# Register-addressed key page fetches on GpSimd, and a later place for the first memory weight's split

## The chip, the core and the metric

The kernel runs on one core of a Trainium2 chip. The metric is the device time of one execution in microseconds (us). A core has a matrix engine (TensorE, PE in the profile; its weight loads are PEld), a vector engine (VectorE, DVE), an activation engine (ScalarE, ACT), GpSimd (POOL), and SyncE (SP), which in this kernel only issues transfers. Each engine works through its own queue in order. The order of each queue is fixed when the program is built, and engines wait for one another by semaphores. Transfers between the main memory and the on-chip memory run on 16 DMA engines and are issued here from SP, POOL and in a few cases ACT.

## The reference: one decoder layer for a prompt and eight samples

A layer of a decoder is computed for a prompt of 512 tokens and for one new token of each of eight sequences that have 1024 cached tokens. What matters here:

```
past = cache_kv_l[page_table]                     # nsa_sample: 8 pages of 128 tokens for each sequence
full = jnp.concatenate([past, new4], axis=1)
kvc = compress_blocks(full[:, :, 0:2], w_cmp, pe_cmp)
...
s_c = jnp.einsum('btghd,bngd->bghtn', qg, kvc[:, :, 0]) * scale      # compressed branch
o_c = jnp.einsum('bghtn,bngd->btghd', p_c.astype(dt), kvc[:, :, 1])
...
o_s = jnp.einsum('bghtkr,bgtkrd->btghd', p_s..., sel[..., 1, :])     # selected branch
...
def mem_project(mem, g_mem, w_xkv):
    return (rmsnorm(mem, g_mem) @ w_xkv).reshape(B, M, 2, X_HEADS, X_HEAD_DIM)
```

The cached keys of a sequence lie in pages in any order, and the page table names them. The attention has a compressed, a selected and a window branch. The memory projection multiplies 256 memory tokens with `w_xkv`; its keys and values are used by the cross-attention of a later stage. A gated feed-forward part follows.

## The kernel before

The work goes in stages. First come the input projections of the normalised tokens (`project`, line 205) with the rounding of each weight into two parts, `w_hi` by ACT and `w_lo`, the difference, by DVE (`split_w`, lines 191 to 195, whose copies are recorded as lines 117 and 120). Between and behind these come the scores of the cached keys (`cached_scores`, from line 658), the sample's softmaxes, the compressed values (`cmp_values`, from 812), the selected values (`selected_values`, from 870) and the pooling group (`pooling`, from 981). From about 174 us on the prompt's attention runs beside the rest of the memory projection and part of the output projection, then cross-attention and the feed-forward part, which takes the larger half of the time.

Several such streams are written as generators, and `merge` takes from them in turn by given weights. This gives the order of the program. A scheduler in the framework then orders each engine's queue when the program is built: of what its own model of the time holds ready, it takes what comes first in the program. `tc.high_priority()` moves instructions ahead, and `tc.issue_after(i)` adds for each instruction of a block on i's engine that it stands behind i in that engine's queue; it adds no semaphore.

*Key pages.* `fetch_keys(b)` (line 327) fetches the keys of sequence b: eight pages, each 128 partitions with 1 KB. For six of the eight sequences SP loads the page numbers from the tile `pages` into registers, with bounds, and issues eight direct transfers with the page number in a register (line 335). For sequences 1 and 2 POOL issues eight indirect transfers (line 337). Those take a row number for each partition from the tile `ix_k`, which DVE works out from the page table and a constant (`row_numbers`, line 323). In the program 0 comes first, then 2, 1 and, in between other work, 3 to 7. Sequence 2's fetch stands under `issue_after(last_square)`, an ACT instruction. The keys of sequences 0 to 3 are first read by `cached_scores(0)` (line 668), those of 4 to 7 by `cached_scores(1)`. POOL also fetches rows of cached values, in the indirect form (`fetch_values`, line 344, tiles `Vcmp` and `Vslc`, row numbers `ix_v`), and stores the first keys and values (line 487).

*Compressed values.* `cmp_values` goes in four rounds q. Each has products with the cached values (line 826), a copy of the result (`pvs`; by DVE for even q, by ACT for odd), four transposes (834), a copy of those (`pv2`, in the profile `pv`; by ACT for even q, by DVE for odd) and products with the compression weight (844). `cmp_last` keeps the last instruction of ACT and of DVE up to that copy, and after the fourth round it names those of that round. The scaling of the memory tokens (`memory_split`, line 1216, tiles `mT_hi`, `mT_lo`) already stands behind these two.

*Memory keys.* `memory_keys(q, banks)` (line 1223) loads a quarter of the key weights, rounds it in two halves with `split_w` and multiplies it (line 1235). Quarter 0 is called at the end of `pooling`, which runs beside `sample_end`. Its buffer `w_raw` is one of two that all weights take in turn, so its transfer (line 181) starts when the weight before has been split. Before the change only the second half of quarter 2 had an order by hand:

```
with tc.issue_after(reduced[0]) if reduced and q == 2 and l else ExitStack():
    w = split_w(raw[:, :, l * P:(l + 1) * P])
```

## Time and profile before

| what | value |
|---|---|
| median of 3 runs | 836.8 us (834.53 to 836.95) |
| the profiled execution's own time | 842.45 us |
| its span, from the first to the last instruction | 840.6 us |
| its mean granted TensorE clock | 0.991 |
| busy in the span: PE, PEld, DVE, ACT, POOL | 813.0, 757.0, 605.4, 448.0, 104.3 us |
| moved by DMA | 137.87 MB, 164 GB/s on the mean |
| POOL indirect transfers of key pages | 16, 1116 ns each on the mean |

A row of a timeline has the start and the duration in us, the engine, the line of the kernel, the operation, the tiles (written <- read), the shape, and how often it is repeated. Brackets at the end give the idle time of the engine just before, and what ended it. "SPq" is the queue that issues transfers. In the chain of waits a row has a start, a duration and what the chain went through. A row of the stage table has a stretch, its length and, for each engine, busy time and number of instructions. "issue" is time in which an engine waited for nothing that the profile shows, "remote" a wait whose releaser it does not know.

### The profile page before, as it was taken

The page shows a single profiled execution, that of the slowest core. Times are in us where ns is not written, and L with a number is a line of the kernel's source. Part 1 is how long each engine was busy: PE and PEld are TensorE (multiplying, and loading weights), DVE is VectorE, ACT ScalarE, POOL GpSimd, SP SyncE. Part 2 cuts the span into 40 slices and gives each one's busy share as a digit, 9 for nine tenths or more (in the row PEclk, how much of TensorE's full clock was granted, in tenths as well). Part 3 has the DMA queues.
Part 4 walks back from the last instruction along what each step waited for, and adds up shares of the span by engine and source line. Part 5 has one row for each costly group of instructions (what it writes and reads, how often), then busy time and mean ns, then how long its engine had stood idle before and what let it go on. Part 6 is the DMA issues. An engine that isn't in the chain of part 4 may idle for free.

```text
span 840.6 us, 17844 instructions
## 1 busy us (share of the span) xinstructions
PE 813.0 (97%) x6889; PEld 757.0 (90%) x6889; DVE 605.4 (72%) x1460; ACT 448.0 (53%) x940; POOL 104.3 (12%) x100
## 2 busy tenths in 40 slices
PE   8889998999999999999999999999999999999996
PEld 7878785887778799999899999999999999999995
DVE  6454395798676767888864599988888888887623
ACT  6543135667765545344444365676665665655542
POOL 2330011000000014000022000211111211200021
PEclk9999999999999999999999999999999999999998
DMA  9976975673321175477624323766686776763422
GB/s 329 251 241 168 400 300 185 206 254 126 102 75 40 38 215 190 133 250 250 204 64 110 92 68 110 162 152 133 152 166 139 158 158 138 149 154 108 168 121 102
DMA packets 146365, 137.87 MB, mean 164 GB/s; under 512 B 6416, under 2 KB 133264, under 8 KB 144088
## 3 DMA queue, kind: packets, MB, share of 16 engines
q1 hardware_dynamic: 127224, 114.63, 43.9%
q0 software_dynamic: 18624, 21.26, 12.1%
q8 instruction: 54, 0.88, 0.4%
q10 hardware_dynamic: 432, 0.84, 0.3%
q14 instruction: 31, 0.25, 0.1%
HBM read 129.56 MB, written 10.69 MB: 167 GB/s over the span
## 4 chain that ended last, share of the span: by engine, by line
PE 84%; DVE 7%; DMA 3%; ACT 2%; issue 2%; another core or an unknown queue 0%; SPq 0%; DVEq 0%; ACTq 0%
PE ps_pp L205 26%; PE ps_pp L1829 15%; PE ps_pp L1890 15%; PE ps_tb L1266 2%; PE ps_o L1158 2%; PE ps_pp L2070 2%; PE ps_t L1890 2%; PE ps_tb L1075 2%; PE ps_sc L1111 2%; PE ps_tf L1143 2%; PE ps_x L1467 1%; PE ps_tb L1235 1%; PE ps_x L1488 1%; DVE w_lo L120 1%; DMA w_raw<-in_w_xkv_dram 1%
## 5 line engine op out<-in xcount | busy, mean ns | idle before, releaser
L1890 PE MATMUL ps_pp<-xm,w_hi 128*128 128x260 f32 x720 | 133.3, 285 | 0.1
L1890 PEld LDWEIGHTS ps_pp<-xm,w_hi 128*128 128x128 f32 x720 | 110.9, 188 | 2.3 <-ACT ext L117 0.3
L117 ACT ACTIVATE w_hi<-w_u 128x512 fp32r<-128x512 f32 (+2 forms) x110 | 72.7, 661 | 66.5 <-PE ps_pp L1890 22.7
L1890 PE MATMUL ps_pp<-xm,w_lo 128*128 128x260 f32 x360 | 101.4, 282 | 0.0
L120 DVE TENSOR_TENSOR w_lo<-w_u,w_hi 128x512 fp32r<-128x512 f32 (+2 forms) x110 | 80.1, 729 | 16.6 <-ACT w_hi L117 15.3
L1890 PEld LDWEIGHTS ps_pp<-xm,w_lo 128*128 128x128 f32 x360 | 67.7, 188 | 0.0
L120 DVE TENSOR_TENSOR hT<-hT,ps_pp 128x520 f32<-128x520 f32 (+1 forms) x44 | 28.3, 644 | 45.0 <-PE ps_pp L205 18.0
L205 PE MATMUL ps_pp<-x_hi,w_hi 128*128 128x260 f32 x288 | 60.0, 286 | 0.0
L205 PE MATMUL ps_pp<-x_hi,w_lo 128*128 128x260 f32 x288 | 59.6, 285 | 0.0
L205 PE MATMUL ps_pp<-x_lo,w_hi 128*128 128x260 f32 x288 | 58.4, 284 | 0.0
L117 ACT ACTIVATE w_hi<-w_raw 128x1024 fp32r<-128x1024 f32 (+1 forms) x38 | 35.0, 922 | 42.2 <-PE ps_pp L205 30.6
L205 PE MATMUL ps_pp<-xn_hi,w_hi 128*128 128x260 f32 x208 | 46.4, 300 | 1.9 <-issue 1.0
L205 PE MATMUL ps_pp<-xn_lo,w_hi 128*128 128x260 f32 x208 | 44.5, 293 | 2.6 <-issue 2.4
L1880 POOL DMA_DIRECT2D w_u<-in_w_up_dram x19 | 24.4, 1285 | 179.5 <-DMA w_u<-in_w_up_dram 106.4
L205 PEld LDWEIGHTS ps_pp<-x_hi,w_lo 128*128 128x128 f32 x288 | 44.9, 188 | 0.6 <-issue 0.4
L205 PE MATMUL ps_pp<-xn_hi,w_lo 128*128 128x260 f32 x208 | 44.2, 293 | 1.3 <-DVE w_lo L120 0.8
L205 PEld LDWEIGHTS ps_pp<-x_hi,w_hi 128*128 128x128 f32 x288 | 44.9, 188 | 0.3
L205 PEld LDWEIGHTS ps_pp<-x_lo,w_hi 128*128 128x128 f32 x288 | 44.5, 188 | 0.4 <-issue 0.4
L1121 ACT ACTIVATE prob<-prob,mx 128x384 f32<-128x384 f32 (+3 forms) x64 | 35.4, 555 | 17.7 <-DVE mx L1119 17.4
L120 DVE TENSOR_TENSOR w_lo<-w_raw,w_hi 128x1024 fp32r<-128x1024 f32 (+1 forms) x38 | 41.4, 1089 | 4.2 <-ACT w_hi L117 3.9
L120 DVE TENSOR_TENSOR w_lo<-raw_x,w_hi 128x512 fp32r<-128x512 f32 (+1 forms) x53 | 35.7, 674 | 10.3 <-ACT w_hi L117 9.6
L117 ACT ACTIVATE w_hi<-raw_x 128x512 fp32r<-128x512 f32 (+1 forms) x53 | 32.8, 619 | 18.2 <-PE ps_pp L1890 13.1
(495 smaller groups left out, 2321.7 us busy)
## 6 DMA issues: line engine op xcount, KB each, us to landing
w_u<-in_w_up_dram SPq DMA_DIRECT2D x57, 256.0 KB
xkr<-in_cache_mem_dram SPq DMA_DIRECT2D x16, 512.0 KB
xvr<-in_cache_mem_dram SPq DMA_DIRECT2D x16, 512.0 KB
raw_x<-in_w_up_dram SPq DMA_DIRECT2D x26, 256.0 KB
Kt<-in_k_t_dram SPq DMA_DIRECT2D x48, 128.0 KB
w_u<-in_w_up_dram SPq DMA_DIRECT2D x10, 512.0 KB
w_u<-in_w_down_dram SPq DMA_DIRECT2D x20, 256.0 KB
w_u<-in_w_up_dram POOLq DMA_DIRECT2D x19, 256.0 KB
```

The lines of the kernel that those rows point to most:

```text
L117: act.activation(o, i, AF.Copy, scale=scale)
L120: (eng or dve).tensor_tensor(o, a, b, op=op)
L205: pe.matmul(o, a[:, k, :], x[:, hf, :], start=(k == 0 and j == 0), stop=(k == kt - 1 and j == 2))
L1075: pe.matmul(ps[:, :HT], a[:, k, :], y[x][:, k, hf, :], start=(k + j == 0), stop=(k == 3 and j == 2))
L1111: pe.matmul(ss_[hl][:, 0:n], Qst[:, h, qc], k[:, g, u, 0:n], start=(u == 0), stop=(u == 1), skip_group_check=True)
L1121: act.activation(p[:, 0:nk], p[:, 0:nk], AF.Exp, bias=mx[:, hh:hh + 1], scale=-1.0, accum_out=sm[:, hh:hh + 1])
L1143: pe.transpose(pt[:, hh * P:(hh + 1) * P], pr[hh][:, kb * P:(kb + 1) * P], ident)
L1158: pe.matmul(po[hp * 64:(hp + 1) * 64, g * 256:(g + 1) * 256], Vtok[:, br, kb, g * 64:(g + 1) * 64], pTs[kb][:, hp * 256:(hp + 1) * 256], s ...
L1266: pe.matmul(ps[i], x[:, k, ts_], w[:, kl, :], start=(k == 0 and j == 0), stop=(k == KT - 1 and j == 2))
L1829: pe.matmul(ps[:, hf, :HT], a[:, k, :], x[:, hf, :], start=(k0 + k + j == 0), stop=(k0 + k == kt - 1 and j == 2))
L1880: pool.dma_start(u[1], b, accum_op=OP.add)
L1890: pe.matmul(ps, a[:, i, :], b, start=(first and i + q == 0), stop=(i == NI - 1 and q == 2), skip_group_check=True)
```

## The change

Two things. The keys of sequences 1 and 2 are fetched by POOL in the form that SP uses: POOL loads the eight page numbers into registers of its own, with the same bounds, and issues eight direct transfers for each sequence. `ix_k` and its DVE operation are gone; `ix_v` stays. And both halves of the split of the first quarter of the memory weight are placed behind the instructions in `cmp_last`, ACT's part behind ACT's and DVE's part behind DVE's. The order that quarter 2 had by hand stays.

```diff
-    ix_k = const.tile([P, 64], I32, name="ix_k")
     ix_v = const.tile([P, 4], I32, name="ix_v")
...
     def row_numbers():
-        for o, i, n, f, c in ((ix_k, pages[:, 0:64], 64, float(P), C_IX), (ix_v, pages[:, 64:68], 4, 8.0, C_IX + 1)):
-            dve.scalar_tensor_tensor(o, i, f, cst[:, c:c + 1].to_broadcast([P, n]), op0=OP.mult, op1=OP.add)
+        dve.scalar_tensor_tensor(ix_v, pages[:, 64:68], 8.0, cst[:, C_IX + 1:C_IX + 2].to_broadcast([P, 4]), op0=OP.mult, op1=OP.add)
 
     def fetch_keys(b):
 
         t = (pair_tile if b < 2 else ring_tile)("Kt").rearrange("p (a x) -> p a x", a=NPG)
-        if b not in (1, 2):
-            _, at = nc.values_load_multi_w_load_instructions(pages[0:1, b * NPG:(b + 1) * NPG], engines=(EN.SP,),
-                                                             min_val=0, max_val=NPHYS - 1)
+        en, q = (EN.Pool, pool) if b in (1, 2) else (EN.SP, sp)
+        _, at = nc.values_load_multi_w_load_instructions(pages[0:1, b * NPG:(b + 1) * NPG], engines=(en,),
+                                                         min_val=0, max_val=NPHYS - 1)
         for a in range(NPG):
-            if b not in (1, 2):
-                sp.dma_start(t[:, a], A["k_t"][bass.ds(at[a], 1)].rearrange("o p x -> (o p) x"))
-                continue
-            pool.indirect_dma_start(out=t[:, a], out_offset=None, in_=A["k_t"].rearrange("n p x -> (n p) x"),
-                                    in_offset=bass.IndirectOffsetOnAxis(ap=ix_k[:, b * NPG + a:b * NPG + a + 1], axis=0))
+            q.dma_start(t[:, a], A["k_t"][bass.ds(at[a], 1)].rearrange("o p x -> (o p) x"))
         Kt[b] = t
...
         for l in range(2):
-            with tc.issue_after(reduced[0]) if reduced and q == 2 and l else ExitStack():
+            with ExitStack() as late_:
+                for i in (reduced if q == 2 and l else cmp_last.values() if q == 0 else ()):
+                    late_.enter_context(tc.issue_after(i))
                 w = split_w(raw[:, :, l * P:(l + 1) * P])
```

## The prediction

> **What bounds the kernel now.** I read the page first: the span and the shares of the chain that ended last.

> ```profile
> span 840.6 us, 17844 instructions
> ...
> PE 84%; DVE 7%; DMA 3%; ACT 2%; issue 2%; another core or an unknown queue 0%; SPq 0%; DVEq 0%; ACTq 0%
> ```

> TensorE carries the chain, so a time in which TensorE stands still is lost time, and a time in which another engine waits is not. Next I asked for the busy time of every engine by stage (columns: stretch, its length, then busy time and number of instructions of PE, PEld, DVE, ACT, POOL, then granted TensorE clock, DMA share, GB/s).

> ```profile
> 124.00:175.00 51.00, 46.17 (x502) 37.74 (x491) 35.54 (x109) 29.06 (x53) 6.95 (x9) 0.97 0.62 202
> 175.00:430.00 255.00, 252.06 (x1943) 219.02 (x1942) 191.02 (x623) 136.52 (x321) 15.88 (x17) 1.00 0.46 147
> ```

> From 175 us on TensorE idles 2.9 us in 255 (255.00 - 252.06). Everything the diff touches lies before that, where there is something to win: 4.8 us idle between 124 and 175, with the clock not fully granted. So I went into that stage with the chain of waits and the timeline of ScalarE (ACT).

> ```profile
> 123.76 1.15 DVE w_lo L120
> 124.92 8.62 DMA w_raw<-in_w_xkv_dram
> ```

> ```profile
> 128.93 0.67 ACT L117 ACTIVATE pl_d<-ps_pp,vec 128x520 f32<-128x520 f32 x1
> 133.65 1.06 ACT L117 ACTIVATE w_hi<-w_raw 128x1024 fp32r<-128x1024 f32 x1 [4.04 <-DMA w_raw<-in_w_xkv_dram]
> 134.61 0.58 ACT L117 ACTIVATE pv<-ps_tb 128x512 f32<-128x512 f32 x1
> ```

> This is the stall that the second half of the diff aims at. The first memory weight is asked for at 124.92, when a buffer came free, and takes 8.62 us. Its rounding (w_hi) stands in ACT's queue ahead of the copy pv of the compressed values. ACT sits idle for 4.04 us, and pv sits behind it. The timeline of TensorE shows what that costs:

> ```profile
> 130.97 0.63 PE L834 MATMUL ps_tb<-cst,pvs 128*128 128x128 f32 x4
> ...
> 131.53 1.06 PE L826 MATMUL ps_tb<-Vcmp,PTc 128*32 128x512 f32 x8
> ...
> 135.24 0.66 PE L844 MATMUL ps_s<-pv,wv 128*64 128x32 f32 x16 [2.65 <-ACT pv L117]
> ...
> 136.50 1.05 PE L834 MATMUL ps_tb<-cst,pvs 128*128 128x128 f32 x4
> ...
> 137.49 1.94 PE L826 MATMUL ps_tb<-Vcmp,PTc 128*32 128x512 f32 x8
> ```

> The source of pv (L834) was done at 131.60. TensorE waited for pv until 135.24, 2.65 us with nothing to do, and then ran the next L834 and L826 in 1.05 and 1.94 us where the same groups had taken 0.63 and 1.06. The granted clock says why:

> ```profile
> 25.00:29.20 4.20, 1.18 (x7) 0.70 (x5) 1.21 (x10) 0.00 (x0) 2.00 (x3) 1.00 1.05 201
> 30.20:33.60 3.40, 3.40 (x18) 3.40 (x17) 1.97 (x6) 2.22 (x3) 0.00 (x0) 0.50 1.02 276
> 45.00:48.40 3.40, 3.40 (x30) 3.40 (x29) 3.13 (x8) 2.79 (x8) 2.79 (x3) 1.00 1.03 333
> 49.20:53.30 4.10, 0.00 (x0) 0.00 (x0) 0.71 (x2) 0.00 (x0) 2.46 (x3) 1.00 0.61 193
> 54.10:57.50 3.40, 3.40 (x17) 3.05 (x15) 2.68 (x4) 3.31 (x8) 0.00 (x0) 0.50 0.83 250
> 132.60:135.20 2.60, 0.00 (x0) 0.00 (x0) 1.57 (x7) 1.55 (x3) 0.00 (x0) 1.00 0.71 294
> 136.00:139.40 3.40, 3.40 (x16) 1.41 (x16) 0.69 (x1) 1.72 (x4) 0.00 (x0) 0.50 0.02 5
> ```

> Three times TensorE stands still for 2.6 to 4.1 us, and each time 3.4 us at half clock follow. Two of the three lie before 60 us, beside POOL work.

> **Part two of the change, the weight behind the compressed values.** It removes the wait of 2.65 us: pv can start when L834 ends, and TensorE has its own work until 132.59 (131.53 + 1.06). If the idle goes, I count the half clock behind it as gone too: 0.42 on L834 (1.05 - 0.63) and 0.88 on L826 (1.94 - 1.06), 1.30 together. So 3.95 us in all.

> [...] The row has a half clock behind 2.6 idle us.

> What it adds: w_hi (1.06 on ACT) and its difference w_lo (1.22 on DVE) now run behind the last copies of the compressed values, at a place where both engines feed the selected branch. These rows show that place:

> ```profile
> 141.76 1.22 DVE L120 TENSOR_TENSOR w_lo<-w_raw,w_hi 128x1024 fp32r<-128x1024 f32 x1
> ...
> 142.99 0.94 POOL L344 DMA_INDIRECT Vslc<-in_v_slc_dram,ix_v  x1 [15.04 <-PE ps_tb L826]
> 143.46 2.91 ACT L128 ACTIVATE mT_hi<-mt,vec 128x256 fp32r<-128x256 f32 x7
> ...
> 151.44 0.42 DVE L114 COPY PTs<-ps_tb 128x256 f32<-128x256 f32 x1 [1.16 <-PE ps_tb L865]
> ...
> 156.65 1.29 ACT L117 ACTIVATE Ksl<-zk 64x512 fp32r<-64x512 f32 x2 [5.27 <-PE ps_s L874]
> 156.74 0.29 DVE L114 COPY oS<-ps_s 128x128 f32<-128x128 f32 x1 [4.21 <-PE ps_s L874]
> ...
> 158.46 0.28 PE L1235 MATMUL ps_pp<-mT_hi,w_hi 128*128 128x256 f32 x1
> ```

> The first product that needs the weight (L1235) starts at 158.46, and before that ACT idles 5.27 and DVE 4.21 us: room for 1.06 and 1.22 at no cost. If the scheduler puts them ahead of the PTs copies instead, those are up to 1.22 us later and TensorE waits that long. Both ends are possible; I take 0.30, near the free end, because the memory scaling (mT) and the PTs copies come earlier in the program and the idle is four times the work. The fetch at 142.99 is released by TensorE (L826) and moves forward with it, so it is not late next. Sum: 3.95 - 0.30 = 3.65 us won; ends 1.43 (2.65 - 1.22) and 3.95.

> **Part one, the key pages.** Removed: one DVE operation and sixteen indirect transfers. Added: on POOL, a wait for the page table, a load of eight page numbers with bounds for each of two blocks, and sixteen direct transfers. No direct POOL transfer with a register stands in this trace; the nearest rows are POOL's plain store (L487) and SP's own fetches with a register (L335), whose queue the change does not touch.

> ```profile
> 15.99 0.22 DVE L325 SCALAR_TENSOR_TENSOR ix_k<-pages,cst 128x64 int32<-128x64 int32 x1
> ...
> 16.50 2.15 POOL L337 DMA_INDIRECT Kt<-in_k_t_dram,ix_k  x1 [15.23 <-DVE ix_k L325]
> ...
> 39.63 0.58 POOL L487 DMA_DIRECT2D out_kv_t_dram<-Vtok  x1 [12.03 <-DVE Vtok L120]
> 40.52 0.99 POOL L337 DMA_INDIRECT Kt<-in_k_t_dram,ix_k  x1 [0.30 <-issue]
> ...
> 50.59 0.94 POOL L337 DMA_INDIRECT Kt<-in_k_t_dram,ix_k  x1 [0.30 <-issue]
> ...
> 18.11 0.56 SPq L406 DMA_DIRECT2D WT<-in_w_cmp_e_dram  x1
> 24.84 9.03 SPq L335 DMA_DIRECT2D Kt<-in_k_t_dram  x8
> ...
> 72.47 1.44 PE L668 MATMUL ps_s<-Kt,QW 128*32 128x64 f32 x88
> ```

> Dearest case for a block: SP's first one, 6.2 us of loading (18.67 to 24.84) and 9.03 of issuing. Two such on POOL after 15.99 end at 46.5 (15.99 + 2 x 15.2). Cheapest: 16 x 0.58 = 9.3 us. Today the second set ends at 51.53 (50.59 + 0.94), and the first reader, L668, comes at 72.47 with no wait for it. So both ends are hidden behind 20 us of cover; only beyond that would it cost a microsecond for each microsecond. Behind POOL's new wait stand the kv store and the transfers, and only L668 waits for those. I take 0 for the issue itself, and 0 for the DVE operation (0.22 beside a TensorE that goes on working).

> **The sum.** The profiled execution took 842.45 us, 1.85 more than its span; 842.45 - 3.65 = 838.8. The three times have a median of 836.8 (834.53 to 836.95), so the profiled one is 5.65 slower; the wait on a weight's arrival has no reason to differ, and I take the difference from the median: 836.8 - 3.65 = 833.15, say **833.1**. About 0.3%, 2.5 us here, is what a measurement can tell from no change.

> **Rivals.**
> *B, the early stalls go too.* These two rows belong to the second one:

> ```profile
> 52.59 0.70 DVE L120 TENSOR_TENSOR ztile<-ps_pp,R 128x520 f32<-128x520 f32 x1 [4.03 <-remote]
> 53.34 0.33 PE L574 MATMUL ps_pp<-xn_hi,wg_hi 128*56 128x260 f32 x1 [4.17 <-DVE ztile L120]
> ```

> The DVE waits 4.03 us for something that the profile cannot name, while POOL's second set of indirect transfers (40.52 to 51.53) runs; the stall at 25 to 29.2 lies beside the first set. If dropping the indirect form cures both, it is 3.02 (4.20 - 1.18) and 4.10 idle, and at half clock 18 and 17 instructions ran where 30 do, 1.36 and 1.47: 9.95 us. Against it: the transfers stay on POOL, in bursts of eight, and the profiled execution is 5.65 slower than the median, so part of these stalls may not exist in the timed runs. Half of it, 5.0, gives 833.15 - 5.0 = 828.2; all of it 823.2. [...] Chance 0.19.
> *C, the order does not do what it says.* The edges only set a place in two queues; the scheduler may put another waiting operation there, or both parts' effects cancel: 836.8. Chance 0.18.
> *E, the wait goes and the half clock stays.* Its 3.4 us follow a wait shorter than they are, so it may have another cause: 2.65 - 0.30 = 2.35, 834.45. [...] Chance 0.10.
> *D, slower: the second block's pages come into the loading rush.* Nothing ties them to the kv store at 39.63; without the index operation they may follow the first set at once.

> ```profile
> 31.49 1.23 DVE L120 TENSOR_TENSOR w_lo<-w_q,w_hi 128x1024 fp32r<-128x1024 f32 x1 [5.18 <-ACT w_hi L117]
> ...
> 36.06 0.40 PE L205 MATMUL ps_pp<-xn_hi,w_hi 128*128 128x260 f32 x2
> ```

> Between 25 and 29.2 the DMA is full at 201 GB/s. One more MB ahead of the query weight costs 5.2 us; that weight is ready at 32.72 and needed at 36.06, so 3.3 are covered and 1.9 are not. If the timed runs lack the stall at 25 us, TensorE is there 4.4 us earlier (3.02 + 1.36) and 6.3 are not covered, with 1.36 of half clock behind them: 833.15 + 7.7 = 840.8. It decides from 3.3 us of delay on; what speaks against it is that today's second set waited too. Chance 0.17.

> **How the numbers follow.** Forecast A, 833.1, has 0.36 (835.4 to 832.9 by its own ends). Faster by over 2.5 us (under 834.3): B and nine tenths of A, 0.52. Within: C, E and the rest of A, 0.31. Slower: D, 0.17. The range reaches from 826.0, between half and the whole of B's price, to 840.0, short of D's dearest; about 0.18 is left out.

> **What would show it.** Right: no idle before L844 of the compressed values, w_hi of the memory weight after the last pvs, granted clock 1.00 around it, ACT's 4.04 gone; transfers L332 as direct ones on POOL that end before 52 us; L668 without a wait. B shows as busy TensorE between 25 and 54 us at full clock, D as a w_q that lands later and a TensorE that waits for its w_lo near 36 us. I am wrong if another wait stands ahead of pv, or if the PTs copies come a microsecond later than TensorE asks for them.

## The result and the profile after

The changed kernel took 827.11 us (median of 5 runs, 826.34 to 830.93), the kernel before 834.53 us (5 runs on the same chip, 832.31 to 836.95). The ratio is 0.9914, with a 95% interval of 0.9885 to 0.9942: 7.2 us faster, between 4.8 and 9.6. The forecast was 833.1 us, with a range of 826.0 to 840.0. Two executions of experiments further below (1568.84 us of first_indirect, 2734.39 us of second_indirect) lie far above all others, and the ratios are those of the runs without them.

The profiled execution took 830.93 us, against 842.45 before. These are the span and the shares of the chain that ended last, on its page:

```profile
span 829.3 us, 17914 instructions
...
PE 85%; DVE 4%; DMA 4%; ACT 3%; issue 1%; SPq 1%; DVEq 0%; POOL 0%; ACTq 0%
```

DVE's share has fallen from 7% to 4%, and "issue" from 2% to 1%. Next come the stretches that were asked of the kernel before, and three new ones around 90 us, with the same columns:

```profile
25.00:29.20 4.20, 4.20 (x38) 4.20 (x37) 3.48 (x18) 2.77 (x3) 0.60 (x2) 1.00 1.01 211
30.20:33.60 3.40, 3.40 (x29) 3.21 (x28) 1.74 (x4) 2.15 (x3) 0.00 (x0) 1.00 1.05 339
45.00:48.40 3.40, 3.39 (x26) 3.19 (x27) 2.58 (x3) 3.33 (x6) 0.00 (x0) 1.00 1.06 384
49.20:53.30 4.10, 4.10 (x33) 3.68 (x32) 0.84 (x2) 0.48 (x2) 0.00 (x0) 1.00 0.52 142
54.10:57.50 3.40, 3.40 (x25) 2.88 (x26) 0.58 (x3) 0.76 (x4) 0.00 (x0) 1.00 0.33 87
84.00:89.40 5.40, 4.22 (x36) 4.13 (x35) 2.48 (x5) 1.55 (x2) 1.77 (x2) 1.00 1.00 416
89.40:92.40 3.00, 0.33 (x3) 0.12 (x2) 0.00 (x0) 0.00 (x0) 0.00 (x0) 1.00 1.00 415
92.40:95.80 3.40, 3.29 (x16) 0.59 (x16) 0.00 (x0) 0.00 (x0) 0.00 (x0) 0.51 1.02 429
```

Both early stalls are gone. From 25.0 to 29.2 TensorE is busy for all 4.20 us, where it was busy for 1.18, and from 49.2 to 53.3 for all 4.10, where it did nothing. Both half clocks behind them are gone too. But there is a new hole from 89.4 to 92.4 with half clock behind it, while the DMA engines are full at 415 GB/s. The timeline of GpSimd shows the new transfers:

```profile
21.00 4.07 POOL L332 DMA_DIRECT2D Kt<-in_k_t_dram  x7 [19.60 <-DMA xrow_s<-in_x_row_s_dram]
25.47 0.54 POOL L332 DMA_DIRECT2D Kt<-in_k_t_dram  x1 [0.41 <-issue]
34.30 0.55 POOL L481 DMA_DIRECT2D out_kv_t_dram<-Vtok  x1 [8.29 <-DVE Vtok L120]
34.91 4.63 POOL L332 DMA_DIRECT2D Kt<-in_k_t_dram  x8
```

Eight direct transfers take 4.63 us (0.58 each, the value of the plain store that I had set as the cheap end). Eight indirect ones had taken 11.1 us (16.50 to 27.60). The second set ends at 39.54.

The third part is the compressed values, first on the timeline of TensorE, then ScalarE's copy and rounding:

```profile
125.22 1.06 PE L820 MATMUL ps_tb<-Vcmp,PTc 128*32 128x512 f32 x8
126.22 0.66 PE L838 MATMUL ps_s<-pv,wv 128*64 128x32 f32 x16
127.27 0.60 PE L828 MATMUL ps_tb<-cst,pvs 128*128 128x128 f32 x4
127.80 1.07 PE L820 MATMUL ps_tb<-Vcmp,PTc 128*32 128x512 f32 x8
...
147.42 0.28 PE L1231 MATMUL ps_pp<-mT_hi,w_hi 128*128 128x256 f32 x1
```

```profile
125.39 0.60 ACT L117 ACTIVATE pv<-ps_tb 128x512 f32<-128x512 f32 x1 [2.08 <-PE ps_tb L828]
...
139.50 1.05 ACT L117 ACTIVATE w_hi<-w_raw 128x1024 fp32r<-128x1024 f32 x1
140.44 0.37 ACT L117 ACTIVATE PTs<-ps_tb 128x256 f32<-128x256 f32 x1
```

No idle stands before L838, and L828 and L820 behind it take 0.60 and 1.07 us, where they had taken 1.05 and 1.94 at half clock. The copy pv now waits for TensorE and no longer for a weight. The rounding w_hi now stands 14 us behind that copy (139.50 against 125.39) and ahead of one PTs copy, and the first product that needs it (L1231) starts without a wait. One short wait is new, for the fetched rows of the selected values:

```profile
141.26 0.63 PE L868 MATMUL ps_s<-Vslc,PTs 128*32 128x128 f32 x12 [0.28 <-DMA Vslc<-in_v_slc_dram,ix_v]
```

The same work can be followed through both executions by the start of TensorE's rows. Times are us; "again" is a profiled execution of the changed kernel from a later session (further below):

| TensorE's row | before | after | difference | again | difference |
|---|---|---|---|---|---|
| first product on Qe and WT | 57.70 | 46.87 | -10.83 | 47.59 | -10.11 |
| first product on the window keys Wk | 99.47 | 92.51 | -6.96 | 91.74 | -7.73 |
| first product on Vcmp | 128.68 | 122.40 | -6.28 | 119.97 | -8.71 |
| first product on mT_hi and the memory weight | 158.46 | 147.42 | -11.04 | 145.60 | -12.86 |
| span | 840.6 | 829.3 | -11.3 | 828.0 | -12.6 |

The early stalls give over 10 us. Between 57 and 128 us 4.55 of them are given back in the one execution, 1.4 in the other. The compressed values give over 4 us more, and after that at most 0.3 us changes. The two profiled executions differ by more than the medians (11.5 us against 7.4): that of the kernel before took 7.9 us more than its median, that of the changed kernel 3.8 us more. So the rows tell where time was won, and only the ratio tells how much.

### The profile page after: what moved, and what is told of

The parts are those of the page before. It is cut to its first block, busy times and chain, and to the rows that moved or that the text cites. A ratio compares the mean times of both kernels' runs of the same rounds, so it can differ in the third digit from the quotient of the medians.

```text
span 829.3 us, 17914 instructions
## 1 busy us (share of the span) xinstructions
PE 809.6 (98%) x6889; PEld 753.9 (91%) x6889; DVE 604.7 (73%) x1459; ACT 448.3 (54%) x940; POOL 95.4 (12%) x100
## 4 chain that ended last, share of the span: by engine, by line
PE 85%; DVE 4%; DMA 4%; ACT 3%; issue 1%; SPq 1%; DVEq 0%; POOL 0%; ACTq 0%
PE ps_pp L205 26%; PE ps_pp L1825 16%; PE ps_pp L1886 15%; PE ps_tb L1262 3%; PE ps_o L1152 2%; PE ps_pp L2066 2%; PE ps_t L1886 2%; PE ps_tb L1069 2%; PE ps_sc L1105 2%; PE ps_tf L1137 2%; DMA Wk<-in_win_k_t_dram 2%; PE ps_x L1463 1%; PE ps_tb L1231 1%; PE ps_x L1484 1%; DMA Vslc<-in_v_slc_dram,ix_v 1%
## 5 line engine op out<-in xcount | busy, mean ns | idle before, releaser
L117 ACT ACTIVATE w_hi<-w_u 128x512 fp32r<-128x512 f32 (+2 forms) x110 | 72.7, 661 | 66.5 <-PE ps_pp L1886 22.8
L120 DVE TENSOR_TENSOR w_lo<-w_u,w_hi 128x512 fp32r<-128x512 f32 (+2 forms) x110 | 80.0, 728 | 16.6 <-ACT w_hi L117 15.3
L120 DVE TENSOR_TENSOR hT<-hT,ps_pp 128x520 f32<-128x520 f32 (+1 forms) x44 | 28.3, 644 | 44.9 <-PE ps_pp L205 17.9
L205 PE MATMUL ps_pp<-x_hi,w_hi 128*128 128x260 f32 x288 | 59.9, 286 | 0.0
L205 PE MATMUL ps_pp<-x_hi,w_lo 128*128 128x260 f32 x288 | 59.6, 285 | 0.0
L205 PE MATMUL ps_pp<-x_lo,w_hi 128*128 128x260 f32 x288 | 58.4, 284 | 0.0
L117 ACT ACTIVATE w_hi<-w_raw 128x1024 fp32r<-128x1024 f32 (+1 forms) x38 | 35.0, 922 | 40.5 <-PE ps_pp L205 26.2
L120 DVE TENSOR_TENSOR w_lo<-w_raw,w_hi 128x1024 fp32r<-128x1024 f32 (+1 forms) x38 | 41.4, 1088 | 8.3 <-ACT w_hi L117 8.2
L205 PEld LDWEIGHTS ps_pp<-x_hi,w_lo 128*128 128x128 f32 x288 | 44.9, 188 | 0.6 <-issue 0.4
L205 PE MATMUL ps_pp<-xn_hi,w_hi 128*128 128x260 f32 x208 | 45.0, 293 | 0.5 <-ACT w_hi L117 0.5
L205 PEld LDWEIGHTS ps_pp<-x_hi,w_hi 128*128 128x128 f32 x288 | 44.8, 188 | 0.3
L205 PEld LDWEIGHTS ps_pp<-x_lo,w_hi 128*128 128x128 f32 x288 | 44.5, 188 | 0.4 <-issue 0.4
L205 PE MATMUL ps_pp<-xn_lo,w_hi 128*128 128x260 f32 x208 | 43.2, 287 | 1.2 <-issue 1.2
L205 PE MATMUL ps_pp<-xn_hi,w_lo 128*128 128x260 f32 x208 | 43.5, 288 | 0.5 <-DVE w_lo L120 0.4
L120 DVE TENSOR_TENSOR w_lo<-raw_x,w_hi 128x512 fp32r<-128x512 f32 (+1 forms) x53 | 35.7, 674 | 10.3 <-ACT w_hi L117 9.6
L117 ACT ACTIVATE w_hi<-raw_x 128x512 fp32r<-128x512 f32 (+1 forms) x53 | 32.8, 618 | 18.2 <-PE ps_pp L1886 13.1
```

Source lines behind the costliest of these rows:

```text
L117: act.activation(o, i, AF.Copy, scale=scale)
L120: (eng or dve).tensor_tensor(o, a, b, op=op)
L205: pe.matmul(o, a[:, k, :], x[:, hf, :], start=(k == 0 and j == 0), stop=(k == kt - 1 and j == 2))
```

## The experiments

Each was timed in a session, on one chip, together with the kernel before. That kernel had medians of 834.5 to 843.3 us in the five sessions, so a comparison across sessions is weak, by ratios as well as by times, and the text says where it makes one.

**1. Each part alone.** For the keys alone, the split stays where it was; for the split alone, the key pages stay indirect.

```diff
 keys_alone (against the changed kernel)
-            with ExitStack() as late_:
-                for i in (reduced if q == 2 and l else cmp_last.values() if q == 0 else ()):
-                    late_.enter_context(tc.issue_after(i))
+            with tc.issue_after(reduced[0]) if reduced and q == 2 and l else ExitStack():
 split_alone (against the kernel before): the same lines the other way
```

> Part one alone: both sets of key pages as direct transfers of GpSimd, the memory weight's split where it was before. Theory 1 (each set of indirect transfers makes a stall of TensorE at its end, in timed runs too, and the window keys' arrival takes part of the gain back): both early stalls of 3.0 and 4.1 us and their half clocks gone, a wait for the window keys of some 3 us near 92 us, the idle of 2.65 us before the compressed values' second product still there; about 3 us faster than the kernel before (7.2 of the whole change less 4.3 of the split). Theory 2 (the early stalls are made by the recording of the trace and the timed runs lack them): no change in time, within 1 us. Theory 3 (the index operation's removal or the split's place frees the early stage): part one alone leaves at least one of the stalls.

> Part two alone: the memory weight's split behind the compressed values, the key pages by indirect transfers as before. Theory 1: both early stalls as before, no idle and full clock at the compressed values, 4.3 us faster (my forecast had 3.65). Theory 2: the whole gain of the change, about 7 us faster.

The keys alone: 0.993 (0.9905 to 0.9955), 5.9 us of 842.0, where about 3 were expected. The split alone: 0.9958 (0.9932 to 0.9983), 3.5 us, where 4.3 were expected. Both parts carry time, so theory 2, under which the early stalls are made by the recording, is out. Of theory 3, the index operation stays open until the next experiment, since it is gone in this kernel too. The split's place is out: the stage view of the keys alone shows both stalls gone without the split.

```profile
25.00:30.00 5.00, 5.00 (x44) 5.00 (x43) 3.40 (x17) 2.96 (x3) 0.97 (x2) 1.00 1.03 183
48.00:54.00 6.00, 6.00 (x46) 5.50 (x47) 1.51 (x3) 1.57 (x4) 0.00 (x0) 1.00 0.55 181
74.20:78.00 3.80, 0.13 (x2) 0.00 (x0) 0.00 (x0) 1.00 (x1) 0.00 (x0) 0.91 0.81 277
```

The timeline of its TensorE shows the two waits that are left, one for a weight of the projections, one before L838:

```profile
78.11 0.80 PE L205 MATMUL ps_pp<-xn_hi,w_hi 128*128 128x260 f32 x2 [3.78 <-ACT w_hi L117]
...
131.26 0.66 PE L838 MATMUL ps_s<-pv,wv 128*64 128x32 f32 x16 [2.35 <-ACT pv L117]
```

So the predicted wait came, but at a weight and not at the window keys. The split alone has the stall at 25 us as before (2.70 busy in 25 to 30) and TensorE busy for 14.06 of the 15 us from 125 to 140, at clock 1.00, where the kernel before has 12.27 at 0.89:

```profile
25.00:30.00 5.00, 2.70 (x15) 2.18 (x15) 1.19 (x10) 0.71 (x1) 2.07 (x3) 0.93 1.04 214
...
125.00:140.00 15.00, 14.06 (x167) 11.03 (x167) 11.83 (x47) 6.88 (x18) 3.40 (x4) 1.00 0.63 233
```

The order in which TensorE's and ScalarE's instructions stand is that of before in the one and that of the changed kernel in the other, so part one does not act by another order of the work.

**2. One set indirect, the other direct.** Both keep the whole of the rest, and have `ix_k` with its DVE operation again.

```diff
 first_indirect (against the kernel before; second_indirect has 1 and 2 exchanged)
-        if b not in (1, 2):
+        en, q = (EN.Pool, pool) if b in (1,) else (EN.SP, sp)
+        if b not in (2,):
...
-            if b not in (1, 2):
-                sp.dma_start(t[:, a], A["k_t"][bass.ds(at[a], 1)].rearrange("o p x -> (o p) x"))
+            if b not in (2,):
+                q.dma_start(t[:, a], A["k_t"][bass.ds(at[a], 1)].rearrange("o p x -> (o p) x"))
```

> The whole change, but the set that comes first (sequence 2) indirect and the other direct; the index operation is back. Theory 1, each burst has its own stall: the stall near 25 to 29 us and its half clock come back, none near 50 us; 1 to 3 us slower than the whole change, so 4 to 6 faster than the kernel before. Rival, the stalls hang on the index operation or on the DMA rush alone: both stalls or none.

> The whole change, but the set that comes second (sequence 1) indirect and the first direct. Theory 1: no stall near 25 us, a stall of about 4 us at the end of the second set, between 40 and 50 us, with half clock behind it; 4 to 6 us faster than the kernel before. Rival: both stalls or none. If the time here and with the first set indirect are both that of the whole change, the stalls are in the traces but not in the timed runs.

Measured: 0.9905 (0.9871 to 0.9939) and 0.9882 (0.9841 to 0.9922), which is 8.0 and 9.9 us. Stage views, the first set indirect, then the second:

```profile
25.00:30.00 5.00, 2.34 (x14) 1.56 (x12) 1.59 (x12) 0.00 (x0) 3.00 (x4) 1.00 1.02 211
30.20:33.60 3.40, 3.27 (x15) 3.29 (x16) 1.05 (x1) 2.96 (x3) 0.00 (x0) 0.51 1.03 321
43.00:48.00 5.00, 5.00 (x44) 5.00 (x43) 4.54 (x9) 4.85 (x14) 2.34 (x5) 1.00 0.99 346
```

```profile
25.00:30.00 5.00, 5.00 (x44) 5.00 (x43) 3.31 (x17) 2.96 (x3) 0.00 (x0) 1.00 1.06 216
...
44.40:47.80 3.40, 1.46 (x9) 0.95 (x7) 0.38 (x1) 0.00 (x0) 1.68 (x3) 1.00 1.05 366
47.80:51.20 3.40, 3.08 (x15) 2.88 (x15) 2.83 (x4) 2.96 (x7) 0.00 (x0) 0.51 0.75 268
```

Each indirect set brings its own stall and half clock, and only its own; the index operation is in both kernels and is not the cause. What the stall looks like stands on TensorE's timeline of the first of them. The profile shows nothing that is waited for; TensorE gets one instruction in 0.7 to 1.4 us:

```profile
26.16 0.31 PE L205 MATMUL ps_pp<-xn_lo,w_hi 128*128 128x260 f32 x1
27.49 0.37 PE L205 MATMUL ps_pp<-xn_lo,w_hi 128*128 128x260 f32 x1 [1.02 <-issue]
28.87 0.28 PE L205 MATMUL ps_pp<-xn_hi,w_lo 128*128 128x260 f32 x1 [1.01 <-issue]
29.60 0.28 PE L205 MATMUL ps_pp<-xn_hi,w_lo 128*128 128x260 f32 x1 [0.44 <-issue]
```

The whole change was not run in that session, so the expected 1 to 3 us can't be read off. A later session gave it 0.9897, by which the kernels with one indirect set would cost nothing, but 827.8 us, by which they would cost 4 to 6. The session itself has a better yardstick, the split alone (0.9958), which has both sets indirect and the rest of the change. Against it the kernel that keeps only the first set indirect is 4.5 us faster, and the one that keeps only the second 6.4 us. The intervals of the first pair still overlap a little, those of the second do not. So making one set direct pays in timed runs too.

**3. Does it need a long burst, and full DMA engines?** Half of the first set indirect; the second set indirect but begun later; and all sixteen direct in one row.

```diff
 half_burst (against first_indirect)
-        en, q = (EN.Pool, pool) if b in (1,) else (EN.SP, sp)
-        if b not in (2,):
+        en, q = (EN.Pool, pool) if b in (1, 2) else (EN.SP, sp)
+        if True:
...
-            if b not in (2,):
+            if b != 2 or a >= 4:
                 q.dma_start(t[:, a], A["k_t"][bass.ds(at[a], 1)].rearrange("o p x -> (o p) x"))
 late_indirect, late_indirect_timed (against second_indirect)
-        for o, i, n, f, c in ((ix_k, pages[:, 0:64], 64, float(P), C_IX), (ix_v, pages[:, 64:68], 4, 8.0, C_IX + 1)):
+        for o, i, n, f, c in ((ix_v, pages[:, 64:68], 4, 8.0, C_IX + 1),):
...
         fetch_keys(2)
-    fetch_keys(1)
...
     run(qt)
+    with last_on(EN.DVE):
+        dve.scalar_tensor_tensor(ix_k, pages[:, 0:64], float(P), cst[:, C_IX:C_IX + 1].to_broadcast([P, 64]), op0=OP.mult, op1=OP.add)
+    fetch_keys(1)
 sixteen_direct (against the changed kernel)
-            pool.dma_start(O["kv_t"][c], z)
+            with last_on(EN.Pool):
+                pool.dma_start(O["kv_t"][c], z)
```

> The whole change, but the first four pages of the first set (sequence 2) are indirect transfers, the other four direct. If the stall needs a long burst (it began 6 to 8 us after a burst's first transfer in four places): none, or under 1 us of idle between 18 and 30 us. If each indirect transfer adds its part: about half of the stall, 1.5 us of idle with slow issue. If the form alone counts: the stall of 3 us.

> The whole change, but the second set (sequence 1) indirect and begun later, when the loading has ebbed (the DMA's share falls from 0.95 to 0.4 to 0.6 between 48 and 58 us). If the stall needs full DMA engines beside the burst: no idle of TensorE above 1 us near the burst's end, full clock. If the burst alone makes it: an issue stall of some 3 us beginning 6 to 8 us after its first transfer. The pages may come late for the scores, which would show as a wait for Kt and is not the stall in question.

> The kernel with sequence 1's set indirect and begun at 46 us, now timed. Theory 1 in its present form (an indirect burst stalls the engines only while the DMA engines are full): within 2 us of the changed kernel on the same chip, on the faster side if anything. Rival (the form costs wherever it stands, and the single time of 825.8 us was a lucky one): 3 us slower than the changed kernel.

> The changed kernel with both sets of GpSimd's direct transfers in one row of sixteen: the stores of the first keys and values are placed behind them. At 0.58 us each the row lasts about 10 us, as long as eight indirect transfers (11.1 us), and falls into the full loading between 20 and 32 us. If the length of a burst in full loading makes the stall: slow issue and 2 to 4 us of idle of TensorE between 25 and 34 us, half clock behind it. If the indirect form makes it: TensorE busy at full clock there. It tests rival D of the prediction too: 1 MB more in the loading rush, priced at 7.7 us if the query weight comes late; without that the time is that of the changed kernel, within 2 us.

The half burst, GpSimd's timeline and then the stages:

```profile
22.07 1.32 POOL L338 DMA_INDIRECT Kt<-in_k_t_dram,ix_k  x1 [20.68 <-DMA xrow_s<-in_x_row_s_dram]
...
27.17 2.24 POOL L336 DMA_DIRECT2D Kt<-in_k_t_dram  x4
```

```profile
24.00:27.00 3.00, 3.00 (x28) 3.00 (x26) 1.73 (x12) 2.20 (x4) 2.39 (x3) 1.00 1.02 181
27.00:30.00 3.00, 3.00 (x28) 3.00 (x27) 1.97 (x6) 1.72 (x2) 2.41 (x5) 1.00 1.07 211
30.00:34.00 4.00, 4.00 (x34) 3.81 (x33) 1.56 (x4) 1.80 (x3) 0.00 (x0) 1.00 1.05 343
```

Four indirect transfers into full DMA engines stall nothing here. Nor do eight that begin at 46.04, when the DMA share is lower; GpSimd's first and last and the stages of the late set:

```profile
46.04 1.04 POOL L338 DMA_INDIRECT Kt<-in_k_t_dram,ix_k  x1 [11.42 <-DVE ix_k L1284]
...
54.92 0.95 POOL L338 DMA_INDIRECT Kt<-in_k_t_dram,ix_k  x1 [0.30 <-issue]
```

```profile
48.00:52.00 4.00, 4.00 (x30) 3.58 (x31) 0.53 (x2) 0.38 (x1) 3.09 (x4) 1.00 0.62 188
52.00:56.00 4.00, 4.00 (x31) 3.48 (x30) 0.47 (x2) 0.55 (x2) 2.95 (x4) 1.00 0.90 288
```

TensorE's first gap came 6.8 to 9.2 us after a burst's first transfer in the six early sets that are indirect (in the kernel before, the split alone and the two of experiment 2). For the late set that would be 52.8 to 55.2 us, where TensorE is busy throughout. The half burst took 831.36 us and the late set 825.78, one time each. Timed, the late indirect set gave 0.9905 (0.9873 to 0.9936), with 0.9897 (0.9871 to 0.9923) for the changed kernel in the same session: no difference. So the indirect form is harmless there. It was seen to cost where eight ran into a DMA that was full (share 1.03 from 45.0 to 48.4 before the second stall). In the split alone it did so at less, too: its second set had a share of 0.90 from 40 to 44 and 0.73 from 44 to 48, and TensorE's gaps began at 46.7. So a full DMA is not shown to be the condition: the share beside the late set is hardly lower (0.62 and 0.90), and TensorE does other work there.

The sixteen did not come in one row: GpSimd waited 5.16 us for a landing ahead of the ninth, which started at 32.18 and not at 26, so the test of length against form did not come about. TensorE was busy throughout (5.00 of 5.00 us and 4.00 of 4.00 in 25 to 30 and 30 to 34), though 1 MB came into the loading 3 us earlier. The time was 828.93 us, within 2 us of the changed kernel's 827.1 and 827.8 in other sessions. The ratio of 0.9824 (0.9793 to 0.9855) is lower because the kernel before took 843.3 there.

**4. What gave part of it back.** In the changed kernel the new hole is a wait for the window keys. The tile's rows after and before (columns: lowest, median and highest ns of one, first and last start), each with the wait that TensorE had for it or none:

```profile
L688 PE MATMUL ps_s<-Wk,Qbd x16: 977/1060/1061, 92.5 to 95.1; 128*32 128x512 f32 x16
...
  PE ps_s L688: 2.8, 1
```

```profile
L694 PE MATMUL ps_s<-Wk,Qbd x16: 592/592/617, 99.5 to 100.8; 128*32 128x512 f32 x16
```

The wait of 2.78 us and the half clock behind it (3.56 us for a group that took 1.92) make 4.4 us, about the 4.55 given back. TensorE came 6.96 us earlier, and the transfer was not there. Two kernels move the loading order:

```diff
 window_first
+    fetch_window_keys()
     raw_p = [None, load_in(2)]
-    fetch_window_keys()
 seven_window: that, and sequence 7's pages on GpSimd
-        en, q = (EN.Pool, pool) if b in (1, 2) else (EN.SP, sp)
+        en, q = (EN.Pool, pool) if b in (1, 2, 7) else (EN.SP, sp)
```

> The changed kernel with two further edits: sequence 7's key pages on GpSimd as direct transfers, and the window keys' transfer ahead of the next weight's in SyncE's queue. Theory 1 (loading gave part of the gain back at the window keys): the wait for the window keys near 92 us (2.8 us with 1.6 us of half clock behind it) goes or shrinks below 1 us, and the time falls 2 to 5 us below the changed kernel, about 11 below the kernel before. Rival (what bounds here is the sum of bytes, 415 GB/s over 76 to 112 us, so that another tile is late instead): the wait moves to a weight or to the window values and the time is that of the changed kernel, within 1.5 us.

> The changed kernel with only the window keys' transfer ahead of the next weight's in SyncE's queue (sequence 7 stays on SyncE). The transfer is issued 1 us earlier of 13.9 at the least. Theory 1: the wait for the window keys shrinks by 1 to 3 us, the time by as much. Rival by the sum of bytes: no change, within 1.5 us of the changed kernel.

Both failed: 0.9976 (0.9958 to 0.9995) and 0.9968 (0.9953 to 0.9984), 2.0 and 2.7 us faster than before, where the changed kernel is 7.2 and 8.6 in its two sessions. The wait for Wk did go in both, and another took its place. For seven_window, TensorE's row is

```profile
85.02 4.01 PE L662 MATMUL ps_s<-Kt,QW 128*32 128x64 f32 x125 [7.05 <-DMA Kt<-in_k_t_dram]
```

and for window_first

```profile
115.23 0.33 PE L798 MATMUL ps_tb<-cst,Pz 128*128 128x128 f32 x1 [3.42 <-DVE Pz L114]
```

In the first, the pages of sequence 7 stood behind 2 MB of window keys; in the second DVE was late, and its chain goes back to a transfer of the pooling state that was under way for 20.54 us. My rival by the sum of bytes named the right kind (another tile is late instead) but gave the time of the changed kernel; by the ratios they are 4 to 7 us slower than that, which rests on a comparison across sessions.

Last, the changed kernel again, and its second set held back to 46 us in the direct form (GpSimd's set then started at 49.70):

```diff
 late_direct (against the changed kernel)
         fetch_keys(2)
-    fetch_keys(1)
...
     run(qt)
+    with last_on(EN.DVE):
+        dve.memset(hold, 0.0)
+    pool.memset(hold, 0.0)
+    with last_on(EN.Pool):
+        fetch_keys(1)
```

> The changed kernel once more, as the yardstick on this chip: a ratio of 0.9885 to 0.9942 to the kernel before. Its profile tells whether the wait of 2.8 us for the window keys near 92 us belongs to every execution (it then comes again at that place) or whether the late tile is another one each time (the loading as a whole is late).

> The changed kernel with sequence 1's set direct as in it, but held back to about 46 us by a small operation of VectorE and GpSimd that adds no work of its size (a memset of 128x2 on each). If the later place of 1 MB is what helps (it leaves the full stretch of 34 to 48 us): 1 to 3 us faster than the changed kernel and the same as the late indirect set. If the place does not matter: the changed kernel's time, within 1 us.

They gave 0.9897 (0.9871 to 0.9923) and 0.9894 (0.9866 to 0.9921): the later place is worth nothing. In the second execution of the changed kernel no wait for Wk is left; TensorE waited for a weight instead:

```profile
76.68 0.51 PE L205 MATMUL ps_pp<-xn_hi,w_hi 128*128 128x260 f32 x2 [2.01 <-ACT w_hi L117]
```

In late_direct it waited 1.82 us for Wk again. So the loading between 70 and 100 us as a whole is what TensorE now meets, and which tile is last differs between executions. No kernel here was shown to be faster than the changed one: the two that were timed together with it equal it, and the lower ratio of sixteen_direct comes with a slower kernel before.

## Why the prediction was right or wrong

**The time lies in the range, but not by the forecast.** The forecast had 3.7 us of gain, from the split alone; measured were 7.2. What brought 827.1 inside was the lower end of the range, and that end was there for rival B.

**The split (part two) was right, and its size nearly.** I had 2.65 of idle and 1.30 of half clock less 0.30 for the new place, 3.65. Between the first product on Vcmp and the first on the memory weight the changed kernel gains 4.76 us (11.04 - 6.28) in the one execution and 4.15 (12.86 - 8.71) in the other; alone the split was measured at 3.5 us (1.4 to 5.7). Two terms were a little off. The 1.30 counted only the groups L834 and L826, and other products of the stretch ran at half clock too: from the first L834 to the third L844 (L828 and L838 after) it is 11.68 us before and 7.40 after, 4.28 less, so 1.63 beside the idle. The 0.30 for the new place was not seen as such, since L1231 does not wait. But the fetch of the selected values, which I had called "not late next", was late by 0.28 us in the one execution and 0.88 in the other. The order came out as written, so C falls.

**E falls.** The half clock went with the idle (L820 at 1.07 us). I had held against the sum that the 3.4 us of half clock follow a wait shorter than they are. They did follow one of only 2.65 us, and they are gone with it all the same; what stood ahead of the other half clocks is in the last section.

**Part one, "0 for the issue itself", failed as the forecast of that part.** The bounds on the issue were right (4.63 us for eight, the cheap end; the second set at 39.54; L668, now L662, without a wait; the 46.5 in the dearest case should be 46.4). But the term for the rest of the part was zero, and measured alone it is 5.9 us (3.8 to 8.0). The mechanism stood there as rival B, with the right place and, in the trace, the right price: 9.95 us, against a lead of 10.83 at the Qe row, 0.42 of which was there before the first stall.

**Two steps kept B at 0.19.** One was "the transfers stay on POOL, in bursts of eight". That a set stays on the same engine and in the same queue is not what matters. The queue table of the two pages, before and after, has the same row:

```profile
q0 software_dynamic: 18624, 21.26, 12.1%
```

The packets and the bytes of that queue are the same in both forms, and that told nothing of the stalls: in this queue eight transfers take 4.63 us in the direct form and 11.1 in the indirect one, and before 60 us TensorE was seen to stall only beside the second (1.18 of 4.20 us busy from 25.0 to 29.2, and all 4.20 after). The other step was "part of these stalls may not exist in the timed runs". The keys alone are faster in timed runs too, so a large part exists there. Set by set, the timed runs give 4.5 us for making the second direct and 6.4 for the first (experiment 2), where I had priced 5.57 and 4.38. These can't be added, since each was measured with the other set still indirect.

**The half of B that I priced at 828.2 was near the result for another reason than the one I gave.** I had halved it because part of the stalls might be missing in timed runs. Both went, and in the traces 1.4 to 4.55 us were given back to loading, a wait that I had named nowhere. That the halved price came near the result is luck.

**D falls.** The second set did come earlier, at 34.91 for 40.52, and in sixteen_direct at 32.18; TensorE had no wait for the query weight in either.

**What stays open.** Why TensorE got so few instructions beside eight early indirect transfers (one in 0.7 to 1.4 us, experiment 2) was not found. Late loading of instructions does not show as the cause: in the kernel before, the two queues that the page calls "instruction" (q8 and q14) moved no packet from 20.3 to 36.9 us and from 43.4 to 58.0, so none during either stall or at its end. Beside four (DMA share 1.02 and 1.07) and beside the late eight (0.62 and 0.90) TensorE was busy throughout; whether it would be beside a direct burst of the same length was not tried, since GpSimd paused. And the gain differs between sessions: the changed kernel, and the variants that leave its loading order between 70 and 100 us as it is and have no early indirect set, had medians of 827.1 to 828.9 us in three sessions, while the kernel before had 834.5 to 843.3 in five. This need not be the chip: two of the sessions were on a chip with the same number in the record, and the kernel before took 842.0 us in one and 836.4 in the other. The parts, measured in one session (5.9 and 3.5), and the whole, measured in others (7.2 and 8.6), can't be added up to better than that.

## What to carry to other kernels

A stall that the profile gives to nothing ("issue", "remote") and that lies at the end of another engine's burst of transfers deserves the weight of its price in the sum: two of the three stalls here were of that kind (9.95 us by the rows, 5.9 us timed), and changing one set at a time settled it. When a stage that is full of loading gets faster, look for the tile that is then late and take off what it gives back; moving one transfer ahead in such a queue only moved the wait here (from 2.78 us for the window keys to 7.05 for the key pages or 3.42 for the pooling). An operation that waits for a late transfer belongs behind the copies that TensorE waits for, in the same queue: for one that waited 4.04 us that was worth 3.5 us here.

## What was not expected of the hardware

```profile
72.70:76.10 3.40, 1.97 (x17) 1.76 (x15) 0.00 (x0) 0.53 (x1) 0.00 (x0) 1.00 0.74 281
76.10:79.50 3.40, 2.31 (x17) 2.10 (x18) 2.84 (x3) 1.58 (x2) 0.00 (x0) 1.00 0.84 255
```

So half clock came behind one wait of 2.65 us, shorter than a step, and behind several short gaps alike. (The first of the three that I had read as standing still is four gaps of 0.43 to 1.14 us.) The busy time of a step does not part the cases sharply: 3.50 us with 1.73 busy had half clock behind them (the split alone, 46.3 to 49.8), and a step with 1.60 had none (late_direct, from 87.2: the last product ends at 88.80, and the next sixteen take 1.92 us as at full clock).

Busy time is not the whole of it. In the split alone a step that was busy throughout is followed by four at half clock (0.50 up to 76 us, 0.73 from 76 to 78):

```profile
60.00:63.40 3.40, 3.40 (x27) 2.98 (x27) 0.42 (x1) 0.24 (x1) 0.00 (x0) 1.00 0.23 64
63.40:66.80 3.40, 3.40 (x17) 3.17 (x16) 0.43 (x1) 0.52 (x2) 0.00 (x0) 0.50 0.82 247
```

TensorE runs narrow products there: 64 or 66 columns wide, or of the shapes 128*32 and 128*56. A busy step of this work had half clock behind it in two more executions (late_indirect_timed, clock 0.65 from 54 to 58 us behind 4.00 of 4.00 busy; sixteen_direct, where the products of 128*32 that take 0.28 us at 55.8 take 0.42 from 58.5 to 61.1); in the kernel before the same work went at full clock (1.00 from 58 to 70 us, busy throughout). What decides was not found. The stretch in the split alone belongs to an execution of 844.77 us, 5.7 above that kernel's median.
